# Feed-forward down products of a two-layer decoder: 512-column matmuls written as pairs of 256 columns

## The chip, the cores and the metric

The kernel runs on one core of a Trainium2 chip. Times are device microseconds (us) of that core for one execution of the whole program. The time of the kernel before is the median of three executions, 1899.12 us (1896.09 to 1910.9).

## The reference

Two post-norm decoder layers on 512 tokens of 1024 features. Each layer is a feed-forward network, a mixer (differential attention in layer 0, causal pooling in layer 1), cross-attention into 256 memory tokens, and a second feed-forward network; each of these is followed by a layer norm. What the change touches are the four feed-forward networks:

```python
def swiglu_ffn(x, w_in, w_out):          # x 512 x 1024, w_in 1024 x 5632, w_out 2816 x 1024
    h = x @ w_in
    g, u = jnp.split(h, 2, axis=-1)
    return (jax.nn.silu(g) * u) @ w_out
...
x = layer_norm(a * x + 0.5 * swiglu_ffn(x, ffn_w_in[i, 0], ffn_w_out[i, 0]), ln_g[i, 0], ln_b[i, 0])
```

## The kernel before

Every number is kept as two parts, hi and lo, and every product of float32 is made of three matmuls: hi x hi, hi x lo, lo x hi. The helper `mm3(out, w, x, ...)` issues them in lines 231, 232 and 233; `w` is loaded into the array (stationary, 128 x 128) and `x` streams through it (moving, 128 rows by the columns of `out`). ScalarE makes the hi parts (tiles wh, ha, hb, xh) and VectorE the lo parts (wl and the others), a split each.

A feed-forward network is one block, `ffn`. Its inner features are cut in eleven units of 256, and products of 2 x 2 blocks are made with seven multiplications instead of eight. `up` computes a unit: in each of its steps one of the seven multiplications, 24 matmuls of 256 columns into a bank x, y or z, with the activations moving (xh, xl, xe) and the weights stationary (wh, wl). Units are worked in turns (`FFN_TURNS`): three in turn 0, then two at a time. `down` takes two finished units back to the 1024 features: in each of its seven steps one multiplication, for two groups of 128 tokens (b = 0, 1) and two units (k = 0, 1), so 12 matmuls, each 512 columns wide, into banks px, py and pz. Here the roles are changed: the weights move (wh, wl) and the activations are stationary (ha, hb). In turns 1 to 4 a step of the block is one step of each of two `up`s and one step of `down`, 48 + 12 matmuls. VectorE adds a bank px, py or pz into the tokens X (line 935).

The last three units (`FFN_LAST`) go through `plain_down` without the seven multiplications: for each of 4 groups of tokens and 2 halves of the output's columns a sum of 18 matmuls of 512 columns in a bank ps, with weights moving and activations (xe) stationary. The weights of the first column half lie in wh and wl, those of the second in tiles hb and ha. Its first two sums are begun beside the last two steps of the last `down`, which have no `up` left beside them. The very last sum of the kernel is already made in two halves of 256 columns. After a sum, VectorE adds it to X and the layer norm of that group of tokens begins.

The order on each engine is the one that a list scheduler makes of the code's order and of pairs named by hand: `queue_behind(a, b)` says that instruction a stands behind b. A flag `at_start` marks the kernel's first block. Tiles of activations and of weights are laid 64 bytes apart modulo 512 in the feed-forward and pooling stages (`APART`), so that a moving and a stationary tile begin at different places.

Of the kernel before, what the change touches and what calls it, by code (L numbers as in the profile page):

```python
# [17 lines left out]
P = 128  # L18
D = 1024
S = 512  # L20
# [26 lines left out]
    turn=(1.0, 1.0, 1.2, 1.5),  # L47
# [12 lines left out]
FFN_LAST = (8, 9, 10)  # L60
# [56 lines left out]
def drain(units):  # L117
    for _ in units:
        pass


def few(units, n):
    for _ in range(n):
        next(units, None)


class Trunk:
# [442 lines left out]
    def ffn(self, layer, j, ln, beside=()):  # L570
        w_in, w_out = self.a["ffn_w_in"][layer, j], self.a["ffn_w_out"][layer, j]
        self.seven_of, self.factors = {}, self.factor_tiles()
        nc, n, beside = self.nc, len(FFN_TURNS), iter(beside)
        at_start = bool(self.load_rest)
        downs = {i: self.down(d, w_out, 2.0 * ALPHA if i == 1 else 1.0) for i, (_, d) in enumerate(FFN_TURNS) if d}

        def start(turn):
            ups = FFN_TURNS[turn][0]

            early = (2, 1, 1) if turn == 0 else (0, 0)  # L580
            rest = self.load_rest.pop if turn == 0 and at_start else lambda: lambda: None
            got = [self.up(w_in, u, lane, early[lane], rest() if lane == 0 else None) for lane, u in enumerate(ups)]
            for lane, g in enumerate(got):
                next(g)
                if lane == 1:
                    rest()()
            if turn > 1:
                next(downs[turn])
            return got + [downs[i] for i in downs if i == turn]

        works = start(0)
        if at_start:

            zeros = self.act("hb", (P, P + S), mybir.dt.bfloat16)
            nc.vector.memset(zeros, 0.0)
            idle = self.aux("idle", "yz")
            self.warm(zeros, idle, 7)
            for tag, half in (("px", 0), ("py", 1)):
                for t in self.late[:2]:
                    self.turn(t, half, tag)  # L600
                if half == 0:
                    with self.tc.issue_after(self.last_turn.ins):
                        self.warm(zeros, idle, 9)
                next(works[0])
                if half == 0:
                    next(works[0])
            next(works[1])
        else:
            for w in works + works[:1]:
                next(w)  # L610
            self.turn_late(2)
        self.late = []
        next(works[0])
        act, dve = self.first_split
        if self.begins:

            for late, first in zip(self.begins, (act, dve)):
                self.queue_behind(late, first)
        second = self.second_factors()
        if at_start:  # L620

            next(works[0])
            for w in (works[1], second, second, works[1], works[2], works[2], works[0]):
                with self.behind():
                    next(w)
        else:
            for w in (second, *works[1:], second, downs[1]):
                next(w)
        for turn in range(n):
            behind = turn == n - 1  # L630
            for step in range(1 if turn == 0 else 0, 9 if behind else 7):
                if turn == 0 and (step == 3 or step == 2 and at_start):
                    next(second)
                if step == 4:
                    if behind:
                        coming = [self.plain_down(w_out, layer, j, ln, beside)]
                    else:
                        coming = start(turn + 1)
                        if at_start and turn == 0:
                            with self.tc.issue_after(self.last_load.ins):  # L640
                                next(downs[1])
                if behind and step in (4, 6, 7, 8):
                    next(coming[0])
                if behind and step > 3:
                    few(beside, 2)

                for lane, w in enumerate(works[: None if not behind or step > 1 else -1]):
                    if not (at_start and turn == 0 and lane < 2 and step == 1):
                        next(w, None)
                    if turn == 0 and lane == 1 and step == 2 and at_start:  # L650
                        next(works[0])
                    if turn == 0 and lane == 0 and step == 2 and not at_start:
                        next(second)
                    if at_start and turn == 0 and lane == 0 and step == 3:
                        next(works[2])
                if turn == 1 and step == 3:
                    self.seven_of[self.waiting[0]] = self.seven(self.waiting[1])
            works = coming
        drain(works[0])
# [63 lines left out]
    def up(self, w, u, lane, early, between):  # L723
# [28 lines left out]
        def product(ps, v, a, start=False, passes=False):  # L752
            if passes or between and start and a == 0:
                by_passes(ps, v, a)
                return
            x = self.factors[a]
            for j in range(2):
                o = slice(j * P, (j + 1) * P)
                for k in range(4):

                    self.mm3(
                        ps[:, j], (v[0][:, k, o], v[1][:, k, o]), (x[0][:, k], x[1][:, k]),
                        start and j == k == 0, j == 1 and k == 3, True,
                    )

        def by_passes(ps, v, a, which=range(3)):

            x = self.factors[a]
            halves = [(n, i, l) for n in range(8) for i, l in ((0, 0), (0, 1))]
            for group in ([halves[:8], halves[8:], [(n, 1, 0) for n in range(8)]][w] for w in which):  # L770
                for n, i, l in group:
                    j, k = divmod(n, 4)
                    self.last_mm = nc.tensor.matmul(  # L773
                        ps[:, j], v[i][:, k, j * P : (j + 1) * P], x[l][:, k],
                        start=n == i == l == 0, stop=n == 7 and i == 1, skip_group_check=True,
                    )
# [5 lines left out]
        at_start = early > 0 and self.begins is None  # L782
# [13 lines left out]
        x = bank(self.aux("x", "px") if third else self.mm("x"))  # L796
# [7 lines left out]
        if at_start and lane == 0:  # L804
            by_passes(x, v, 0, (1, 2))
        else:
            product(x, v, 0, True, third and at_start)
# [6 lines left out]
        with self.behind() if at_start else nullcontext():  # L814
            if early > 1 and not at_start:
                wide = v2[0][:, :2].rearrange("p k n -> p (k n)")
                for _ in range(2):
                    nc.tensor.matmul(
                        y.rearrange("p j n -> p (j n)"), v2[0][:, 0, :P], wide, start=True, stop=True
                    )  # L820
            product(y, v2, 1, True, lane != 1 and at_start)
# [47 lines left out]
        if u in FFN_LAST:  # L869
            h = self.act("xe", (P, 2, S)), self.act("xe", (P, 2, S))  # L870
# [25 lines left out]
    def down(self, pairs, w, scale):  # L896
# [14 lines left out]
        hs = [self.seven_of[u] for u in pairs]  # L911

        def operand(raw):
            t = self.hl([P, 2, S])
            self.split(t[0], t[1], raw)
            return [(t[0][:, i], t[1][:, i]) for i in range(2)]
# [4 lines left out]
        def product(ps, b, a, ws, start=False):  # L921

            o = slice(b * P, (b + 1) * P)
            for k in range(2):
                h, l = hs[k][a]
                self.mm3(ps, (h[:, o], l[:, o]), ws[k], start and k == 0, k == 1, not start)

        started = set()

# [8 lines left out]
        ws = operand(b11)  # L938
# [7 lines left out]
        ws = operand(b21)  # L946
        for b in B:
            ps = self.aux("py", "py")
# [3 lines left out]
        ws = operand(b11)  # L952
# [8 lines left out]
        ws = operand(b22)  # L961
# [4 lines left out]
        ws = operand(b11)  # L966
# [5 lines left out]
        ws = operand(b12)  # L972
# [4 lines left out]
        ws = operand(b11)  # L977
# [5 lines left out]
    def plain_down(self, w, layer, j, ln, beside):  # L983
# [8 lines left out]
        ws = [[], []]  # L992
# [15 lines left out]

        def product(ps, half, t, k, n=slice(0, S)):
            o = slice(t * P, (t + 1) * P)  # L1010
            for c in range(2):
                h = [x[:, c, o] for x in self.seven_of[FFN_LAST[k]]]
                self.mm3(ps, h, [x[c][:, n] for x in ws[half][k]], k == c == 0, k == 2 and c == 1)

        operand(0, 0)
        yield
# [2 lines left out]
        for n, (half, t) in enumerate(LAST):  # L1019
# [14 lines left out]
            ps = self.aux("ps", ("yz", "py")[n % 2])  # L1034
# [788 lines left out]
```

## Time and profile before

| | |
|---|---|
| median of three runs | 1899.12 us |
| profiled execution | 1899.25 us, of which the profile's span is 1897.5 us |
| TensorE busy | 1886.5 us, 13120 matmuls |
| weight loads busy | 1730.9 us |
| VectorE busy | 1540.9 us |
| ScalarE busy | 1000.8 us |
| GpSimd busy | 308.2 us |
| memory read and written | 274.79 and 4.19 MB |

Busy times of engines overlap each other. A matmul's busy time contains its pipeline, so that the next one starts before it ends: what a matmul costs in a run of them is the time from its start to the next one's start.

### The profile page before, as it was taken

The page shows a single profiled execution, that of the slowest core. Times are in us where ns is not written, and L with a number is a line of the kernel's source. Part 1 is how long each engine was busy: PE and PEld are TensorE (multiplying, and loading weights), DVE is VectorE, ACT ScalarE, POOL GpSimd, SP SyncE. Part 2 cuts the span into 40 slices and gives each one's busy share as a digit, 9 for nine tenths or more (in the row PEclk, how much of TensorE's full clock was granted, in tenths as well). Part 3 has the DMA queues.
Part 4 walks back from the last instruction along what each step waited for, and adds up shares of the span by engine and source line. Part 5 has one row for each costly group of instructions (what it writes and reads, how often), then busy time and mean ns, then how long its engine had stood idle before and what let it go on. Part 6 is the DMA issues. An engine that isn't in the chain of part 4 may idle for free.

```text
span 1897.5 us, 32589 instructions
## 1 busy us (share of the span) xinstructions
PE 1886.5 (99%) x13120; PEld 1730.9 (91%) x13120; DVE 1540.9 (81%) x2246; ACT 1000.8 (53%) x1542; POOL 308.2 (16%) x274
## 2 busy tenths in 40 slices
PE   9999999999999999999999999999999999999998
PEld 8999998888889988999998999999899889999996
DVE  7888989888876558889887988898786568998886
ACT  6555554566654435555554655555455436555552
POOL 3112120112110002221220311212120012211210
PEclk9999999999999999999999999999999999999999
DMA  9978772322235327987785687777464438867861
GB/s 254 215 178 178 171 141 85 103 69 75 91 112 178 112 70 181 195 177 168 144 188 168 118 179 181 168 166 162 157 172 146 142 69 180 173 159 178 185 129 53
DMA packets 250055, 283.20 MB, mean 149 GB/s; under 512 B 8752, under 2 KB 213040, under 8 KB 249904
## 3 DMA queue, kind: packets, MB, share of 16 engines
q0 software_dynamic: 94080, 94.38, 32.3%
q1 hardware_dynamic: 155824, 186.74, 30.2%
q8 instruction: 103, 1.69, 0.4%
q14 instruction: 48, 0.39, 0.1%
HBM read 274.79 MB, written 4.19 MB: 147 GB/s over the span
## 4 chain that ended last, share of the span: by engine, by line
PE 96%; DMA 2%; DVE 1%; ACT 0%; SPq 0%; issue 0%; POOL 0%; DVEq 0%; ACTq 0%
PE x L231 7%; PE x L232 7%; PE x L233 7%; PE ps L231 5%; PE ps L233 4%; PE ps L232 4%; PE z L231 4%; PE z L233 4%; PE z L232 4%; PE px L233 3%; PE px L231 3%; PE px L232 3%; PE x L773 3%; PE y L231 2%; PE y L232 2%; PE y L233 2%
## 5 line engine op out<-in xcount | busy, mean ns | idle before, releaser
L741 POOL DMA_DIRECT2D ra<-in_ffn_w_in_dram x132 | 170.7, 1307 | 977.6 <-DVE wl L748 960.4
L746 ACT CAST wh<-ra 128x1024 fp32r<-128x1024 f32 x176 | 184.9, 1053 | 197.8 <-PE x L232 63.8
L748 DVE TENSOR_TENSOR wl<-ra,wh 128x1024 fp32r<-128x1024 f32 x176 | 214.2, 1220 | 64.7 <-ACT wh L746 64.0
L231 PE MATMUL x<-xe,wh 128*128 128x256 f32 x704 | 195.0, 277 | 0.0
L232 PE MATMUL x<-xe,wh 128*128 128x256 f32 x704 | 194.8, 277 | 0.0
L233 PE MATMUL x<-xe,wl 128*128 128x256 f32 x704 | 194.8, 277 | 0.0
L746 ACT CAST wh<-rc 128x1024 fp32r<-128x1024 f32 x132 | 138.9, 1053 | 100.3 <-PE x L232 41.6
L143 ACT CAST wh<-b 128x1024 fp32r<-128x1024 f32 x112 | 117.8, 1052 | 134.8 <-PE x L232 62.2
L748 DVE TENSOR_TENSOR wl<-rc,wh 128x1024 fp32r<-128x1024 f32 x132 | 159.5, 1218 | 24.7 <-ACT wh L746 24.7
L144 DVE TENSOR_TENSOR wl<-b,wh 128x1024 fp32r<-128x1024 f32 x112 | 136.7, 1220 | 40.9 <-ACT wh L143 40.9
L231 PE MATMUL x<-xh,wh 128*128 128x256 f32 x536 | 148.7, 277 | 0.0
L232 PE MATMUL x<-xl,wh 128*128 128x256 f32 x536 | 148.4, 277 | 0.0
L233 PE MATMUL x<-xh,wl 128*128 128x256 f32 x536 | 148.4, 277 | 0.0
L231 PEld LDWEIGHTS x<-xe,wh 128*128 128x128 f32 x704 | 132.4, 188 | 1.3
L232 PEld LDWEIGHTS x<-xe,wh 128*128 128x128 f32 x704 | 132.3, 188 | 1.3
L233 PEld LDWEIGHTS x<-xe,wl 128*128 128x128 f32 x704 | 132.2, 188 | 0.0
L144 DVE TENSOR_TENSOR wl<-raw,wh 128x1024 fp32r<-128x1024 f32 x64 | 78.5, 1233 | 45.8 <-ACT wh L143 45.2
L231 PEld LDWEIGHTS x<-xh,wh 128*128 128x128 f32 x536 | 100.8, 188 | 0.7
L232 PEld LDWEIGHTS x<-xl,wh 128*128 128x128 f32 x536 | 100.8, 188 | 0.7
L233 PEld LDWEIGHTS x<-xh,wl 128*128 128x128 f32 x536 | 100.7, 188 | 0.0
L143 ACT CAST wh<-raw 128x1024 fp32r<-128x1024 f32 x64 | 66.4, 1049 | 62.5 <-PE xq L232 18.2
L231 PE MATMUL z<-xe,wh 128*128 128x256 f32 x352 | 97.5, 277 | 0.0
(445 smaller groups left out, 6239.9 us busy)
## 6 DMA issues: line engine op xcount, KB each, us to landing
ra<-in_ffn_w_in_dram POOLq DMA_DIRECT2D x132, 512.0 KB, 7.0
rc<-in_ffn_w_in_dram SPq DMA_DIRECT2D x88, 512.0 KB, 5.8
b<-in_ffn_w_out_dram SPq DMA_DIRECT2D x76, 512.0 KB, 5.0
ra<-in_ffn_w_in_dram SPq DMA_DIRECT2D x44, 512.0 KB, 4.7
rc<-in_ffn_w_in_dram POOLq DMA_DIRECT2D x44, 512.0 KB, 7.3
raw<-in_xa_wkv_dram SPq DMA_DIRECT2D x16, 1024.0 KB, 5.4
raw<-in_da_w_qkv_dram SPq DMA_DIRECT2D x24, 512.0 KB, 3.7
raw<-in_xa_wq_dram SPq DMA_DIRECT2D x8, 1024.0 KB, 5.2
```

The lines of the kernel that those rows point to most:

```text
L143: self.nc.scalar.copy(hi, src),
L144: self.nc.vector.tensor_sub(lo, src, hi.bitcast(F32)),
L231: self.first_mm = mm(out, w[0], x[0], start=start, stop=False, skip_group_check=again)
L232: mm(out, w[0], x[1], start=False, stop=False, skip_group_check=again)
L233: self.last_mm = mm(out, w[1], x[0], start=False, stop=stop, skip_group_check=again)
L741: nc.gpsimd.dma_start(t, source(*block), accum_op=ALU.add)
L746: hi = nc.scalar.copy(v[0], raw)
L748: lo = nc.vector.tensor_sub(v[1], raw, v[0].bitcast(F32))
L773: self.last_mm = nc.tensor.matmul(ps[:, j], v[i][:, k, j * P : (j + 1) * P], x[l][:, k], start=n == i == l == 0, stop=n == 7 and i == 1, s ...
```

## The change

`down` makes each 512-column product as two of 256 columns: all matmuls of the left half first (both units), then those of the right half, in the same bank. `plain_down` does the same with its sums. One down step of each block stays 512 wide, the first one of turn 1 (in the kernel's first block the first one of turn 2 as well): `ahead` marks it. The first matmul of that step is moved: the up product that stands before it is told, from its fourth group of three matmuls on, to stand behind that first matmul, which puts fifteen up matmuls behind it. 1842 of the wide matmuls become 3684 of 256 columns, so the program has 14962 matmuls instead of 13120, and as many more weight loads; 1522 stay wide.

```diff
@@ ffn
+                self.ahead = step == 0 and 0 < turn < 2 + at_start
                 for lane, w in enumerate(works[: None if not behind or step > 1 else -1]):
@@ up: product
             x = self.factors[a]
+            self.up_mms = []
...
                         start and j == k == 0, j == 1 and k == 3, True,
                     )
+                    self.up_mms.append(self.first_mm)
@@ down: product
             o = slice(b * P, (b + 1) * P)
-            for k in range(2):
-                h, l = hs[k][a]
-                self.mm3(ps, (h[:, o], l[:, o]), ws[k], start and k == 0, k == 1, not start)
+            cols = (0, S) if self.ahead else (0, 2 * P, S)
+            for c, e in zip(cols, cols[1:]):
+                for k in range(2):
+                    h, l = hs[k][a]
+                    self.mm3(
+                        ps[:, c:e], (h[:, o], l[:, o]), [w[:, c:e] for w in ws[k]],
+                        start and c == k == 0, k == 1 and e == S, True,
+                    )
+                    if self.ahead and b == k == 0:
+                        self.queue_behind(self.up_mms[-5], self.first_mm)
@@ plain_down: product
             o = slice(t * P, (t + 1) * P)
-            for c in range(2):
-                h = [x[:, c, o] for x in self.seven_of[FFN_LAST[k]]]
-                self.mm3(ps, h, [x[c][:, n] for x in ws[half][k]], k == c == 0, k == 2 and c == 1)
+            for i in range(0, n.stop - n.start, 2 * P):
+                m = slice(n.start + i, n.start + i + 2 * P)
+                for c in range(2):
+                    h = [x[:, c, o] for x in self.seven_of[FFN_LAST[k]]]
+                    self.mm3(
+                        ps[:, i : i + 2 * P], h, [x[c][:, m] for x in ws[half][k]],
+                        k == c == i == 0, k == 2 and c == 1 and m.stop == n.stop, True,
+                    )
```

TensorE's order in a middle down step (the second step of turn 1 in the first block), before. Each row is line, operation, output <- moving, stationary, with the tiles' numbers, and the output's size.

```order
L233 MATMUL y_1092<-xh_86,wl_1094 128x256
L231 MATMUL py_1128<-wh_1124,ha_883 128x512
L232 MATMUL py_1128<-wl_1125,ha_883 128x512
L233 MATMUL py_1128<-wh_1124,ha_884 128x512
L231 MATMUL py_1128<-wh_1124,ha_929 128x512
L232 MATMUL py_1128<-wl_1125,ha_929 128x512
L233 MATMUL py_1128<-wh_1124,ha_930 128x512
L231 MATMUL py_1136<-wh_1124,ha_883 128x512
```

The same place now:

```order
L233 MATMUL py_1128<-wh_1124,ha_884 128x256
L231 MATMUL py_1128<-wh_1124,ha_929 128x256
L232 MATMUL py_1128<-wl_1125,ha_929 128x256
L233 MATMUL py_1128<-wh_1124,ha_930 128x256
L231 MATMUL py_1128<-wh_1124,ha_883 128x256
L232 MATMUL py_1128<-wl_1125,ha_883 128x256
L233 MATMUL py_1128<-wh_1124,ha_884 128x256
```

The bank py_1128 is written by six matmuls of its left half and then by six of its right half, which load the same stationary tiles a second time. The up products before and behind keep their places.

TensorE's order at the first step of turn 1 in the first block (px gathers the down product, x the last up product before it), before:

```order
L231 MATMUL x<-xh,wh 128x256
L232 MATMUL x<-xl,wh 128x256
L233 MATMUL x<-xh,wl 128x256
L231 MATMUL px<-wh,ha 128x512
L232 MATMUL px<-wl,ha 128x512
L233 MATMUL px<-wh,ha 128x512
```

And now:

```order
L231 MATMUL x<-xh,wh 128x256
L232 MATMUL x<-xl,wh 128x256
L233 MATMUL x<-xh,wl 128x256
L231 MATMUL px<-wh,ha 128x512
L231 MATMUL x<-xh,wh 128x256
L232 MATMUL x<-xl,wh 128x256
L233 MATMUL x<-xh,wl 128x256
```

One wide matmul stands between the third and the fourth group of three of that up product; fifteen up matmuls follow it, and then the other eleven wide ones (L232 and L233 of px first).

TensorE's order near the end of the last block, where the second of the sums (ps) is begun and the last `down` comes back to its bank px, before:

```order
L231 MATMUL ps_20795<-wh_20677,xe_20184 128x512
L232 MATMUL ps_20795<-wl_20678,xe_20184 128x512
L233 MATMUL ps_20795<-wh_20677,xe_20185 128x512
L231 MATMUL px_20407<-wh_20777,hb_19564 128x512
L232 MATMUL px_20407<-wl_20778,hb_19564 128x512
```

And now, with other numbers for the same tiles:

```order
L231 MATMUL ps_22505<-wh_22357,xe_21804 128x256
L232 MATMUL ps_22505<-wl_22358,xe_21804 128x256
L233 MATMUL ps_22505<-wh_22357,xe_21805 128x256
L231 MATMUL px_22039<-wh_22475,hb_21100 128x256
L232 MATMUL px_22039<-wl_22476,hb_21100 128x256
```

The scheduler still puts three matmuls of that sum ahead of px and the rest behind its step; they are now three of twelve halves instead of three of six. On VectorE and ScalarE the same instructions stand in a slightly other order within the blocks (a weight split some places ahead of or behind an addition); on GpSimd and SyncE nothing moves.

## The prediction

> **What bounds the kernel now.** I read the page first (busy time, granted clock, the chain that ended last), then what TensorE waited for, then the order of time inside one feed-forward block.
>
> ```profile
> PE 1886.5 (99%) x13120; PEld 1730.9 (91%) x13120; DVE 1540.9 (81%) x2246; ACT 1000.8 (53%) x1542; POOL 308.2 (16%) x274
> PEclk9999999999999999999999999999999999999999
> PE 96%; DMA 2%; DVE 1%; ACT 0%; SPq 0%; issue 0%; POOL 0%; DVEq 0%; ACTq 0%
> ...
> PE idle L138 <- DVE hb L595: 1.3, 1, 1.3
> PE ps L231 <- DVE X L380: 0.8, 1, 0.8
> ```
>
> The last two lines are the longest in the list of TensorE's waits (us in total, times, longest). TensorE is 99% busy at the full clock and holds 96% of the chain. What counts is therefore the spacing of matmul starts, and the change touches exactly that. In the rows below (start in us, length, instruction) the length overlaps its successor, so I divide the time between two starts by the number of matmuls between them. In "x<-xe,wh" xe streams through the array (moving) and wh is loaded into it (stationary).
>
> ```profile
> 85.09 0.39 PE L231 MATMUL py<-wh,ha 128*128 128x512 f32 x1
> ...
> 87.84 0.28 PE L231 MATMUL z<-xh,wh 128*128 128x256 f32 x1
> ...
> 88.54 0.28 PE L231 MATMUL z<-xh,wh 128*128 128x256 f32 x1
> ...
> 93.30 0.39 PE L231 MATMUL pz<-wh,hb 128*128 128x512 f32 x1
> ...
> 232.93 0.39 PE L231 MATMUL px<-wh,hb 128*128 128x512 f32 x1
> ```
>
> One down step, 12 wide matmuls, takes 85.09 to 87.84: 229 ns each. The next six 256-column matmuls take 0.70 us (117 ns each), the following 42 take 4.76 us: 113.3 ns. So a 256-column matmul has two paces here, **quick** (113.3) and **slow** (about 117.7), and after each wide step the up products need some six matmuls to find the quick one. From 85.09 to 232.93 there are 18 such steps of 12 + 48 matmuls, 8.213 us each. In 256-column matmuls at the quick pace a step would be 72 x 113.3 = 8.160 us. **The prize is 0.053 us a step**, half of it in the wide matmuls themselves (2.75 against 2.72 us), half in the six that follow.
>
> **Which pace the new halves take.** This decides the sum, and no split down product stands in the trace. The nearest are the pooled products: 256 columns, with weights moving and activations stationary as in a down step.
>
> ```profile
> 1417.95 0.36 PE L231 MATMUL ps<-wh,pooled 128*128 128x256 f32 x1
> ...
> 1418.39 0.28 PE L231 MATMUL ps<-wh,pooled 128*128 128x256 f32 x1
> ...
> 1421.81 0.28 PE L233 MATMUL ps<-wh,pooled 128*128 128x256 f32 x1
> 1421.92 0.29 PE L231 MATMUL pk<-mem0h,wh 128*128 128x256 f32 x1
> ...
> 1422.17 0.28 PE L233 MATMUL pk<-mem0h,wl 128*128 128x256 f32 x1
> ...
> 1422.51 0.28 PE L233 MATMUL pk<-mem0h,wl 128*128 128x256 f32 x1
> 1422.62 0.28 PE L231 MATMUL ps<-wh,pooled 128*128 128x256 f32 x1
> ...
> 1425.99 0.28 PE L231 MATMUL ps<-wh,pooled 128*128 128x256 f32 x1
> ...
> 1427.36 0.28 PE L231 MATMUL pk<-mem4h,wh 128*128 128x256 f32 x1
> ...
> 1427.71 0.28 PE L231 MATMUL pk<-mem6h,wh 128*128 128x256 f32 x1
> ```
>
> Entered after transposes and a wait (1417.95 has a longer first matmul), 29 of them from 1418.39 to 1421.81 take 117.9 ns each: slow, to the end. Entered from a quick run of pk, 12 of them from 1425.99 to 1427.36 take 1.37 us, 114.2 ns each: quick, with under 0.02 us lost at the seam. So the pace is handed on, not bound to the operands. At the seam back, a slow run becomes quick (1421.92 to 1422.17: 0.25 us for two, then 0.34 for three, about 0.015 us lost in all); the one quick run that returned to pk went on slowly (1427.36 to 1427.71: three in 0.35 us).
>
> Bounds for a pair of halves are then 226.6 ns (quick) and 235.8 (slow) against 229 now: 2.4 won or 6.8 lost on each of the 1842 products that are split. I take the quick end for down steps that lie between up products, since they are entered from 42 quick matmuls without a wait, and the slow end wherever a wait or transposes come before.
>
> A rule of the Trainium skill ("TensorE: Matmul & The Clock Gate", section "Back-to-back issue gap") speaks against the change: columns/2.4 + 2.5 ns per matmul, so a split product would pay one more fixed 2.5 ns. By it 1842 products cost 4.6 us more, an estimate. The row on 1869.03 below bears on it: wide products at their best take 226.7 ns, two quick halves 226.6, so no fixed part is left; and both stand well over the rule's 215.8 and 109.2.
>
> **The tail of a block.** The last of its steps run without up products beside them, and then come the sums.
>
> ```profile
> 1852.31 1.27 DVE L935 SCALAR_TENSOR_TENSOR X<-X,px 128x512 f32<-128x512 f32 x2
> ...
> 1852.79 0.40 PE L233 MATMUL ps<-wh,xe 128*128 128x512 f32 x1
> 1853.14 0.47 PE L231 MATMUL px<-wh,hb 128*128 128x512 f32 x1
> 1853.45 0.40 PE L232 MATMUL px<-wl,hb 128*128 128x512 f32 x1
> ...
> 1869.03 0.39 PE L231 MATMUL ps<-hb,xe 128*128 128x512 f32 x1
> ...
> 1873.11 0.40 PE L231 MATMUL ps<-wh,xe 128*128 128x512 f32 x1
> ...
> 1877.24 0.40 PE L231 MATMUL ps<-hb,xe 128*128 128x512 f32 x1
> ...
> 1881.37 0.40 PE L231 MATMUL ps<-wh,xe 128*128 128x512 f32 x1
> ...
> 1885.51 0.28 PE L231 MATMUL ps<-hb,xe 128*128 128x256 f32 x1
> ...
> 1889.10 0.29 PE L231 MATMUL ps<-ha,xe 128*128 128x256 f32 x1
> ```
>
> At 1853.14 px is written again, and TensorE first waits until VectorE has read it (the first of two additions from 1852.31, 1.27 us together, ends about 1852.95): 0.35 us from 1852.79 where 0.23 would do. Arriving earlier only lengthens that wait. Behind it nothing restores the quick pace: I expect slow halves. The sums of the second column half (hb and ha moving) are dearer still: the only ones already in halves, 30 matmuls from 1885.51 to 1889.10, take 119.7 ns each, 239.4 a pair. Wide, they take 226.7 (18 from 1869.03 to 1873.11) or 229.4 (18 from 1877.24 to 1881.37), 228.1 in the mean. Sums of the first half take 229.4 wide (18 from 1873.11 to 1877.24).
>
> **The change part by part**, against the profiled execution's 1899.25 us (span 1897.5 and 1.75 around it), which is 0.13 above the median 1899.12:
> - Down steps: 7 steps x 4 turns x 4 blocks = 112. Five stay wide; of the others, three a block (12) have no up products behind them, and 95 do. 95 x 0.053, less 0.004 a step for two seams: **-4.7 us**.
> - The first of those three, with the sums begun beside it, ends in the wait above, which eats its gain: 0. The other two, slow: 24 x 117.9 = 2.83 us for 2.75: 8 x 0.08 = **+0.6**.
> - First-half sums behind the wait, about 251: +6.4 ns each: **+1.6**.
> - Second-half sums, 72 in three blocks and 54 in the last, whose final sum was already in halves: 270 x 11.3 ns = **+3.1**.
> - The wide product moved fifteen matmuls ahead, five times: it interrupts an up run, which then needs its six matmuls once more: 5 x 0.026 = **+0.1**. It reads only hi parts; in the first block ScalarE has its wh ready at 70.16, 6.7 us before the step began (76.83), and 1.7 us earlier still finds it there:
>
> ```profile
> 69.12 1.04 ACT L143 CAST wh<-b 128x1024 fp32r<-128x1024 f32 x1
> ...
> 76.83 0.40 PE L231 MATMUL px<-wh,ha 128*128 128x512 f32 x1
> ```
>
> - 1842 more weight loads and matmuls, no DMA, no more work on VectorE or ScalarE. Where additions and splits change places on VectorE, what hides them is the up products. The tightest split in a down step is this one:
>
> ```profile
> 141.09 1.21 DVE L144 TENSOR_TENSOR wl<-b,wh 128x1024 fp32r<-128x1024 f32 x1
> ...
> 142.58 0.39 PE L231 MATMUL py<-wh,ha 128*128 128x512 f32 x1
> 142.81 0.39 PE L232 MATMUL py<-wl,ha 128*128 128x512 f32 x1
> ```
>
> It ends at 142.30, half a us before the matmul that reads it; with halves that one comes 0.12 us sooner, and 0.39 us is left. In the new order this split stands earlier or keeps its place in most turns. Cost 0; without that cover a wait of some 0.3 us would also lose the pace.
>
> Sum: -4.7 + 0.6 + 1.6 + 3.1 + 0.1 = **+0.7 us**, so 1900.0 for such an execution, and 1900 as the median. What the down steps win, the sums give back.
>
> **The rivals.**
> - *Quick everywhere.* The sums, too, come out quick: 521 of them x -2.4 = -1.3, and the middle keeps -4.7: -6 us, **1893**. For it: the pace is handed on. Against: waits and transposes in the tail, and the slow 30 matmuls from 1885.51.
> - *Half the down steps slow.* The seam from up to down isn't alike in all steps (in the address of the stationary tile behind it), and the trace has only two quick seams of one kind. A slow step pays 24 x 4.6 = 0.11 and 0.015 at the way back, where 0.053 went before: +0.07. 48 slow, 47 quick: +1.1, with the tail's 5.4: +6.5, **1906**.
> - *Slower: halves cost 235.8 everywhere.* Place: the down steps; price: +0.07 each, 95 x 0.07 = +6.7, with the tail +12: **1911**. It decides as soon as the pace drops at the first matmul of each step. For it: most rows with weights moving are slow. If each matmul carries a fixed cost, that is its mechanism too. The skill's 2.5 ns, by itself, would make it 1904.
> - *The up products lose it as well*, as at 1427.36: a quick down step, then 48 slow up matmuls (0.22 us), a slow step (0.11), then quick again: +0.24 for two steps, 95/2 x 0.24 = 11.4, with the tail +17: **1916**.
> - *The change isn't there* (the scheduler moves things back): excluded, its order on TensorE shows the halves and the moved product.
>
> **How the numbers follow.** Chances: forecast 0.40, quick everywhere 0.13, half slow 0.17, all slow 0.14, up products slow too 0.09, something else (new waits, other stages entered in another pace) 0.07. Range 1892 to 1912: from quick everywhere to all slow, leaving out the last two, 0.16. A measurement of this kernel tells about 1%, 19 us, from no change (its three runs go from 1896 to 1911). Every case priced above lies within that; over 1% slower takes the up products' case and waits together, 0.06; over 1% faster 0.02, since all the spacing over 113.3 in these parts is some 10 us.
>
> **What would show it.** Middle of a block: steps of 72 matmuls in 8.16 us, with 113.3 in py, pz and px. If those show 118, the third rival; if the matmuls behind them do, the fourth. Tail: ps at 118 (wh moving) and 120 (hb, ha moving); at 113 there, the first rival. The wait before px at the tail longer by 0.05 us. Wrong altogether if TensorE's list shows new waits for VectorE of some us.

## The result and the profile after

The changed kernel takes **1926.24 us** (median; 1924.81 to 1928.94), the kernel before 1897.51 us in the same comparison: ratio 1.0142, 95% interval 1.012 to 1.0163. That is 28.7 us slower, where the prediction said 1900 and at most 1912. The profiled span grew by 27.4 us, from 1897.5 to 1924.9. Of all executions behind the numbers of this document one was far off, 5531 us in the run with 448 bytes below; it enters no ratio.

The page of the changed kernel, in the lines that answer to those shown of before (busy time, granted clock, and the shares of the chain that ended last):

```profile
PE 1906.2 (99%) x14962; PEld 1825.6 (95%) x14962; DVE 1542.0 (80%) x2246; ACT 999.9 (52%) x1542; POOL 308.0 (16%) x274
...
PEclk9999999999999999999999999999999999999999
...
PE 92%; DVE 3%; DMA 2%; issue 1%; ACT 1%; SPq 0%; POOL 0%; DVEq 0%; ACTq 0%; POOLq 0%
```

TensorE is still 99% busy, and its mean granted clock is 0.999 in both profiled executions. VectorE now holds 3% of the chain where it held 1%, and TensorE's waits have new names at the top (us in total, times, longest):

```profile
PE px L231 <- DVE X L945: 2.3, 4, 1.3
PE ps L232 <- DVE wl L144: 1.9, 2, 1.3
PE pp L1443 <- DVE pooled L144: 1.3, 2, 0.7
PE ps L232 <- DVE hb L144: 1.3, 1, 1.3
```

To see where the 27.4 us stand, I cut both traces at the same matmuls (first down product of a block, first up product behind the step that stays wide, last down steps, end of the sums) and subtract:

| after minus before, us | block 1 | block 2 | block 3 | block 4 | sum |
|---|---|---|---|---|---|
| ahead of the down steps: stages between blocks, turn 0, the wide step | +1.0 | +0.3 | +2.4 | +4.6 | +8.2 |
| middle: the steps of turns 1 to 4 with up products | +3.3 | +2.8 | +2.8 | +2.8 | +11.6 |
| tail: the last down steps and the sums | +2.6 | +1.3 | +2.5 | +1.1 | +7.5 |

About 18 of the 27.4 us are pace, that is spacing of matmul starts without a wait: the middles (11.6), the first turn of block 3 (2.4) and some 3.9 of the tails. The rest is waits and the smaller pieces of the first row. The +1.0 there for block 1 can't be put down to the change: up to that block's first sum the kernel with the down steps alone (below) has the same instructions in the same order on every engine, and it shows -1.1. In its profiled execution 242 matmuls late in turn 0 take 27.43 us, 113.3 ns each; the same 242 take 28.50 us in that of the changed kernel, 117.8 each.

**The middle.** The timeline of TensorE in the first block (start in us, length, instruction), the first matmul of each run:

```profile
83.35 0.28 PE L231 MATMUL y<-xh,wh 128*128 128x256 f32 x1
...
86.07 0.28 PE L231 MATMUL py<-wh,ha 128*128 128x256 f32 x1
...
88.79 0.28 PE L231 MATMUL z<-xh,wh 128*128 128x256 f32 x1
...
94.45 0.28 PE L231 MATMUL pz<-wh,hb 128*128 128x256 f32 x1
...
97.28 0.28 PE L231 MATMUL z<-xe,wh 128*128 128x256 f32 x1
...
102.73 0.28 PE L231 MATMUL pz<-wh,hb 128*128 128x256 f32 x1
...
105.45 0.28 PE L231 MATMUL x<-xe,wh 128*128 128x256 f32 x1
```

24 up products to 86.07 take 113.3 ns each, and the 24 halves of the down step to 88.79 take 113.3 too: the step is entered quick and stays quick. But the 48 up products behind it (to 94.45) take 117.9, and the next 24 halves (to 97.28) 117.9. Then 48 up products to 102.73 take 113.5, the first of them slow, and the next halves 113.3. Steps go **two by two**, quick and slow. Two of them, 88.79 to 105.45, take 16.66 us; two of before take 16.43.

**The wide product that moved ahead**, first block:

```profile
134.58 0.28 PE L231 MATMUL x<-xh,wh 128*128 128x256 f32 x1
...
136.34 0.40 PE L232 MATMUL px<-wl,ha 128*128 128x512 f32 x1
...
138.88 0.28 PE L231 MATMUL y<-xh,wh 128*128 128x256 f32 x1
```

The fifteen up products behind it, quick before, take 1.76 us, 117.3 each; the eleven remaining wide matmuls take 231 each.

**The tail**, last block:

```profile
1878.84 0.28 PE L233 MATMUL ps<-wh,xe 128*128 128x256 f32 x1
1879.45 0.36 PE L231 MATMUL px<-wh,hb 128*128 128x256 f32 x1 [0.34 <-DVE X L945]
...
1885.99 0.28 PE L231 MATMUL ps<-wh,xe 128*128 128x256 f32 x1
...
1891.43 0.28 PE L231 MATMUL ps<-hb,xe 128*128 128x256 f32 x1
...
1895.75 0.28 PE L231 MATMUL ps<-hb,xe 128*128 128x256 f32 x1
```

From start to start the gap before px is 0.61 us. A quick half needs 0.11 of that, so 0.50 is wait. Before it was 0.35 behind a wide matmul, which needs 0.23: a wait of 0.12. Behind the wait the first two sums are quick (48 in 5.44 us, 113.3), and the sums of the second half are at 120.0 (36 in 4.32). Blocks 2 and 3 begin their tails alike; in block 1, whose tail is entered slowly, those 48 take 117.8 each.

**Ahead of block 4** most of the loss is no pace but a wait: in layer 1's pooling stage TensorE waits, in four gaps that hold 3.5 us beyond its usual spacing, for VectorE's splits, VectorE for ScalarE's, and ScalarE for a weight from memory. The same cast of that weight on ScalarE, before:

```profile
1396.34 1.05 ACT L143 CAST wh<-raw 128x1024 fp32r<-128x1024 f32 x1 [3.10 <-DMA raw<-in_xa_wkv_dram]
```

and after:

```profile
1420.53 1.05 ACT L143 CAST wh<-raw 128x1024 fp32r<-128x1024 f32 x1 [8.90 <-DMA raw<-in_xa_wkv_dram]
```

ScalarE stands idle 8.90 us for it instead of 3.10.

### The profile page after: what moved, and what is told of

Same layout as the page of the kernel before. It is cut to its first block, busy times and chain, and to the rows that moved or that the text cites. A ratio compares the mean times of both kernels' runs of the same rounds, so it can differ in the third digit from the quotient of the medians.

```text
span 1924.9 us, 36256 instructions
## 1 busy us (share of the span) xinstructions
PE 1906.2 (99%) x14962; PEld 1825.6 (95%) x14962; DVE 1542.0 (80%) x2246; ACT 999.9 (52%) x1542; POOL 308.0 (16%) x274
## 4 chain that ended last, share of the span: by engine, by line
PE 92%; DVE 3%; DMA 2%; issue 1%; ACT 1%; SPq 0%; POOL 0%; DVEq 0%; ACTq 0%; POOLq 0%
PE x L232 7%; PE x L231 7%; PE x L233 7%; PE ps L231 4%; PE ps L232 4%; PE ps L233 4%; PE z L232 4%; PE z L231 4%; PE z L233 4%; PE px L231 3%; PE px L233 3%; PE px L232 3%; PE x L776 3%; PE y L231 2%; PE y L232 2%; PE y L233 2%
## 5 line engine op out<-in xcount | busy, mean ns | idle before, releaser
L233 PE MATMUL x<-xe,wl 128*128 128x256 f32 x704 | 196.1, 279 | 0.0
L232 PE MATMUL x<-xe,wh 128*128 128x256 f32 x704 | 196.1, 279 | 0.0
L143 ACT CAST wh<-b 128x1024 fp32r<-128x1024 f32 x112 | 117.9, 1053 | 137.0 <-PE x L232 68.0
L233 PE MATMUL x<-xh,wl 128*128 128x256 f32 x536 | 149.4, 279 | 0.0
L232 PE MATMUL x<-xl,wh 128*128 128x256 f32 x536 | 149.4, 279 | 0.0
L233 PEld LDWEIGHTS x<-xe,wl 128*128 128x128 f32 x704 | 132.4, 188 | 0.0
L232 PEld LDWEIGHTS x<-xe,wh 128*128 128x128 f32 x704 | 132.2, 188 | 0.0
L231 PE MATMUL px<-wh,hb 128*128 128x256 f32 x384 | 107.1, 279 | 2.3 <-DVE X L945 2.3
L233 PE MATMUL px<-wh,hb 128*128 128x256 f32 x384 | 106.5, 277 | 0.0
L232 PE MATMUL px<-wl,hb 128*128 128x256 f32 x384 | 106.5, 277 | 0.0
```

Of the source, the lines that this page charges most:

```text
L143: self.nc.scalar.copy(hi, src),
L231: self.first_mm = mm(out, w[0], x[0], start=start, stop=False, skip_group_check=again)
L232: mm(out, w[0], x[1], start=False, stop=False, skip_group_check=again)
L233: self.last_mm = mm(out, w[1], x[0], start=False, stop=stop, skip_group_check=again)
```

## The experiments

All are compared with the kernel before on the same chip. "Theory" in the expectations is: a 256-column matmul runs at one of two paces, about 113.3 and 117.7 ns, and hands its pace on.

**Down steps alone.** The changed kernel with the sums wide again.

```diff
@@ plain_down: product (back as before)
+            for c in range(2):
+                h = [x[:, c, o] for x in self.seven_of[FFN_LAST[k]]]
+                self.mm3(ps, h, [x[c][:, n] for x in ws[half][k]], k == c == 0, k == 2 and c == 1)
```

> The changed kernel with the last output sums left 512 columns wide; only the down steps are in halves (one step of each block wide, first product fifteen ahead). Theory (the pace is handed from matmul to matmul, and a quick down step hands a slow one to the up products behind it): the middles of the blocks take 216.3 us each as in the changed kernel (213.5 before), alternating 113 and 118 ns from step to step, +11 to +12 us in all; the tails return to about 40.5, 40.4, 39 and 38.7 us plus 0.2 each; total 1909 to 1915. Rival (each product in halves carries a fixed cost, 27 us / 1842 = 15 ns): 1284 products cost +19 us, 1916 to 1918, spread evenly over the steps. Second rival (the loss sits in new waits for VectorE): the middles stay at 213.5 and the total comes near 1900.

1915.66 us, ratio 1.0085 (1.0068 to 1.0101). The alternation is there without the halved sums:

```profile
96.20 0.28 PE L231 MATMUL z<-xe,wh 128*128 128x256 f32 x1
...
101.86 0.28 PE L231 MATMUL pz<-wh,hb 128*128 128x256 f32 x1
...
104.69 0.28 PE L231 MATMUL x<-xe,wh 128*128 128x256 f32 x1
```

48 up products in 5.66 us and 24 halves in 2.83: 117.9 both. Middles +2.8 us a block as after, in the first block +4.4 with a new wait before py (a start-to-start gap of 1.2 us). Tails +4.0 in sum, half of it one longer wait before px in the first block (a 2.5 us gap, 0.5 before). The time is a little over the theory's range, by those waits. It is just under the range of the rival with a fixed cost, so the time alone doesn't decide against it. The rows do: that rival spreads its cost evenly over the steps, and these go from 113.4 to 117.9 and back.

**Sums alone.** The kernel before, its sums in halves.

```diff
@@ plain_down: product
+            for i in range(0, n.stop - n.start, 2 * P):
+                m = slice(n.start + i, n.start + i + 2 * P)
...
+                        ps[:, i : i + 2 * P], h, [x[c][:, m] for x in ws[half][k]],
```

> The kernel before with only the last output sums in halves; down steps wide, no product moved. Theory: the middles stay at 213.46 us; the tails grow by 1.1 to 1.4 us each from the pace (118 ns with weights of the first half moving, 120 with those of the second), since nothing brings the quick pace back behind the wait for VectorE; whether the waits in the tails and in the pooling stage of layer 1 (about 3 and 4 us in the changed kernel) come from these sums too is open: total 1902 without them, 1909 with them. Rival (fixed cost of 15 ns a product): 558 products, +8 us, 1905 to 1906, with no product at its old 227 to 229 ns a pair.

1915.77 us, ratio 1.0094 (1.0074 to 1.0113): far over both. Tails +5.6 in sum. The rest stands elsewhere: block 3, which is the same as before up to its sums, is slow from its beginning (+2.4 ahead of its down steps, +5.6 in its middle), and the stages ahead of block 4 lose 4.1. Block 3, TensorE:

```profile
1131.00 0.28 PE L231 MATMUL y<-xh,wh 128*128 128x256 f32 x1
...
1136.65 0.40 PE L231 MATMUL py<-wh,ha 128*128 128x512 f32 x1
...
1139.42 0.28 PE L231 MATMUL z<-xh,wh 128*128 128x256 f32 x1
```

48 up products at 117.7 and 12 wide ones at 231, step after step: 8.42 us where before took 8.213. So the kernel before has a slow course of its own: here a wide step entered slowly hands the slow pace on, and all steps of the block stay there. That isn't so for every wide step entered slowly: the first one of the kernel before (76.83 to 79.63, 233 each) is entered at 118 too, and the up products behind it are quick after four. Block 3 follows block 2 at once, and its turn 0 stood at 117.8 here and after the full change too.

**Another distance.** The changed kernel with `APART` 256 in place of 64 in the feed-forward stage.

```diff
-APART, ROUND, LINE = {"ffn": 64, "da": 448, "pool": 64}, 512, 480
+APART, ROUND, LINE = {"ffn": 256, "da": 448, "pool": 64}, 512, 480
```

> The changed kernel with tiles of activations and weights laid 256 bytes apart modulo 512 in the feed-forward stages, not 64, so that a moving tile stands as far from a stationary one in a down step as in an up product. Theory (the seam is one-sided because the distance is 64 one way and 448 the other): the alternation goes; all middle steps have one pace, 113 (middles near 211.5 us, total 1915 or less) or 118 throughout (middles near 219, total 1935). Rival (the seam loses the pace whatever the distance, because there a weight tile follows itself at the same place): steps still alternate, middles 216 us, total about 1925.

1968.51 us, ratio 1.0363 (1.0348 to 1.0379).

```profile
90.17 0.28 PE L231 MATMUL z<-xh,wh 128*128 128x256 f32 x1
...
95.93 0.28 PE L231 MATMUL pz<-wh,hb 128*128 128x256 f32 x1
...
98.81 0.28 PE L231 MATMUL z<-xe,wh 128*128 128x256 f32 x1
```

48 up products in 5.76 us, 24 halves in 2.88: **120.0 ns all of them**, up and down alike, no alternation. One pace was expected, this value was not. The instructions and their order are the same on every engine and only addresses moved, so where tiles lie sets the pace. That it is the moving tile's place against the stationary one's is the nearest reading. The edit also moves both against tiles that other engines use, and no run kept these apart. 120.0 is also what the tail's hb and ha products take, whose tiles begin 0 apart from xe (modulo 512).

**Second token group wide.** Down steps alone, each step's second group (b = 1) left wide, so that wide matmuls stand ahead of the up products.

```diff
-            cols = (0, S) if self.ahead else (0, 2 * P, S)
+            cols = (0, S) if self.ahead or b == 1 else (0, 2 * P, S)
```

> As the first of these (sums wide), and in each down step only the first group of 128 tokens is in halves; the second group's six matmuls stay 512 wide, so that up products follow a wide matmul as before. Theory: the halves are entered from quick up products and take 113.3 ns, the up products behind need six matmuls for the quick pace as before, so a step gains 14 ns: middles 213.1 us, total 1 to 2 us below before (1895 to 1897). Rival (halves cost more by themselves): 642 products in halves x 7 to 15 ns, +4 to +10 us.

1899.68 us, ratio 1.0005 (0.9995 to 1.0014).

```profile
841.67 0.28 PE L231 MATMUL px<-wh,hb 128*128 128x256 f32 x1
...
843.03 0.39 PE L231 MATMUL px<-wh,hb 128*128 128x512 f32 x1
...
844.40 0.28 PE L231 MATMUL x<-xh,wh 128*128 128x256 f32 x1
...
849.87 0.28 PE L231 MATMUL px<-wh,hb 128*128 128x256 f32 x1
```

Twelve halves at 113.3, six wide at 228, and the up products are back at 114.0 in the mean: the alternation is gone, and the middles of blocks 2 to 4 are 0.32 us each *under* before, the gain the theory gave. So splitting costs nothing here by itself; the seam from halves back to up products does. The first block lost 1.4 in its middle and 1.3 in its tail to new waits for VectorE, hence the miss of the range.

**The same in every step**, with no step wholly wide and none moved ahead.

```diff
-                self.ahead = step == 0 and 0 < turn < 2 + at_start
+                self.ahead = False
```

> Every down step of the kernel before, its first token group (b = 0) in halves and its second (b = 1) wide; no step wholly wide, no product moved ahead, sums wide as before. Theory (the pace is handed on, and a wide group at a step's end is what lets the up products behind it settle on the quick pace): 12 halves at 113.4 ns in each step in the place of 6 wide matmuls at 229, 0.014 us a step, so the middle of each block some 0.33 us shorter, and with VectorE's order as before 1896 to 1897. Rival (the halves themselves bring the first block's waits for VectorE that the run with the moved step showed, 1.5 us before py and 1.3 us before px): 1898 to 1900.

1898.95 us, ratio 0.9998 (0.9989 to 1.0008). Middles -0.32 us in all four blocks, -1.3 together; the first block's tail takes back 0.8 and the stages behind it 1.0, while 0.7 is won ahead of the first down step, where executions of the same instructions differ by more than that. The total lies in the rival's range and not in the theory's. The theory had the pace right; of the rival's two waits the one before px came (a gap of 1.28 us, 0.50 before), the one before py did not. The wait in that tail is this one:

```profile
297.19 0.36 PE L231 MATMUL px<-wh,hb 128*128 128x256 f32 x1 [0.88 <-DVE X L945]
```

So the best use of halves found here equals the kernel before and doesn't beat it.

**First token group wide** instead of the second.

```diff
-            cols = (0, S) if self.ahead else (0, 2 * P, S)
+            cols = (0, S) if self.ahead or b == 0 else (0, 2 * P, S)
```

> Down steps with the first token group wide and the second in halves (the other way round than in the run with the second group wide); the one step of each block wide and moved, sums wide. Theory (what stands at the step's end decides what the up products behind it do): halves behind wide matmuls are slow, as the 30 halves behind the wide sums at the kernel's end were, and slow halves hand the up products the quick pace: 12 x 117.8 for 6 x 229 ns, some 0.02 us a step more than before, 1899 to 1902. If the halves settle on the quick pace behind the wide ones, all 48 up products behind each step are slow, 0.2 us a step: 1917 to 1920. Rival (only the number of halves counts, not which group has them): up products quick and halves quick, 1897 to 1900, as with the second group wide.

1913.03 us, ratio 1.0072 (1.0048 to 1.0095).

```profile
94.74 0.28 PE L231 MATMUL pz<-wh,hb 128*128 128x256 f32 x1
...
96.10 0.28 PE L231 MATMUL z<-xe,wh 128*128 128x256 f32 x1
...
101.75 0.40 PE L231 MATMUL pz<-wh,hb 128*128 128x512 f32 x1
...
103.16 0.28 PE L231 MATMUL pz<-wh,hb 128*128 128x256 f32 x1
...
104.57 0.28 PE L231 MATMUL x<-xe,wh 128*128 128x256 f32 x1
...
110.02 0.39 PE L231 MATMUL px<-wh,hb 128*128 128x512 f32 x1
```

As many halves as with the second group wide, but two by two again: halves 113.3, up products 117.7, six wide at 235, halves 117.5, and then up products at 113.5. What stands last in the step decides, so the rival that only counts halves falls. My own forecast (halves behind wide ones are slow) falls as well: in this run wide matmuls hand on the pace that they got. The forecast's other case (halves quick, and the up products behind every step slow) holds for every other step only.

**The roles exchanged.** The changed kernel with 448 bytes in place of 64: up products then have the distance that down products had, and the other way round.

```diff
-APART, ROUND, LINE = {"ffn": 64, "da": 448, "pool": 64}, 512, 480
+APART, ROUND, LINE = {"ffn": 448, "da": 448, "pool": 64}, 512, 480
```

> The changed kernel with the feed-forward tiles of activations and weights 448 bytes apart modulo 512 in the place of 64, so that the roles of the one that comes first are exchanged. Theory (a seam between up and down products drops or lifts the pace by the order in which the two tiles lie): steps still go two by two between 113 and 118 ns, with the drop now at the other seam (into the down step or back), 1918 to 1932. Rival (each distance has one pace of its own, as 256 bytes had 120 ns): one pace for all and no alternation, 1893 if it is 113 ns, 1950 if it is 118.

1930.39 us, ratio 1.0155 (1.0132 to 1.0179).

```profile
94.26 0.28 PE L231 MATMUL pz<-wh,hb 128*128 128x256 f32 x1
...
96.99 0.28 PE L231 MATMUL z<-xe,wh 128*128 128x256 f32 x1
...
102.43 0.28 PE L231 MATMUL pz<-wh,hb 128*128 128x256 f32 x1
...
105.26 0.28 PE L231 MATMUL x<-xe,wh 128*128 128x256 f32 x1
...
110.92 0.28 PE L231 MATMUL px<-wh,hb 128*128 128x256 f32 x1
```

Halves quick (24 in 2.73 us), up products behind them still quick (48 in 5.44); then the drop: halves 117.9, up products 117.9 (5.66). **The drop has moved to the seam into the down step**, and the seam back holds. The theory gave that, and the time. The time holds 1.5 us of another kind: in the first block's tail, behind a gap of 2.35 us before px, the granted clock is 0.50 from 304.8 to 308.2, and fifteen halves take 213 ns each.

**Both on the same side.** The changed kernel with ha and hb 128 bytes on, so that the moving tile has the same distance from the stationary one (-64) in up and in down products. The same edit was made to two more kernels: all down steps in halves with wide sums, and the kernel before, all wide.

```diff
@@ phase_pool
+                elif t == "_h":
+                    self.pad(ctx, 2 * self.apart)
@@ ffn_phase
-        bufs = dict(b1=1, b3=1, b2=1, b4=1, _x=0, xe=6, hb=4, sp=4, ha=4, sr=1, hr=3)
+        bufs = dict(b1=1, b3=1, b2=1, b4=1, _x=0, xe=6, _h=0, hb=4, sp=4, ha=4, sr=1, hr=3)
```

> The changed kernel with the down products' stationary tiles (ha, hb) laid 128 bytes on instead of 0, modulo 512, so that the moving tile lies 64 bytes behind the stationary one in up products and in down products alike; before, it lay 64 bytes behind in up products and 64 ahead in down products. Theory (the pace changes only at a seam where that order turns over, as the runs with 64 and with 448 bytes showed at opposite seams): no alternation inside a block; 72 matmuls of a step all at 113.3 ns, middles 5 us under the kernel before instead of 11.6 over it, 1906 to 1912 in all; if a block is entered slowly and nothing turns it over, it is slow to the end, 7 us a block, up to 1945. Rival (the seams' drop comes from the change of operands, not from where they lie): two by two as before, 1924 to 1928.

> The same laying of ha and hb (128 bytes on), all down steps in halves without a wide or a moved one, and the sums wide as in the kernel before. Theory: steps of 8.16 us, middles 5 us under the kernel before, of which the first block's waits for VectorE take back 1 to 3: 1893 to 1896. Slow throughout: 1920 to 1928. Rival (the operands, not where they lie): two by two, 1913 to 1917 like the run with the down steps alone.

> The kernel before, all wide, with the same laying of ha and hb (128 bytes on). Theory: without a seam that turns over, the up products behind a wide step need no six matmuls to find the quick pace: 0.026 us a step, some 2.6 us in all, 1894 to 1896; if the pace is slow at a block's start it stays slow, wide matmuls too, 5.6 us a block, up to 1920. Rival (the six slow matmuls come from the wide ones, not from where the tiles lie): no change, 1897 to 1899.

1919.23 us (ratio 1.0107, 1.0092 to 1.0123), 1909.82 (1.0059, 1.0046 to 1.0072) and 1915.20 (1.0087, 1.0073 to 1.0101). The first of them (the added lines shift the line numbers by two):

```profile
96.25 0.29 PE L233 MATMUL z<-xe,wh 128*128 128x256 f32 x1
...
101.71 0.28 PE L233 MATMUL pz<-wh,hb 128*128 128x256 f32 x1
...
104.54 0.29 PE L233 MATMUL x<-xe,wh 128*128 128x256 f32 x1
```

48 up products at 113.8, 24 halves at 117.9, in *every* step: now both seams turn the pace, down at the way in, up at the way back, and a middle is 1.75 us over before (2.98 in the first block). Where down steps are in halves with wide sums, the middles are 1.76 over in each block, the same. The all wide kernel, whose instructions are those of before:

```profile
92.42 0.39 PE L233 MATMUL pz<-wh,hb 128*128 128x512 f32 x1
...
95.21 0.28 PE L233 MATMUL z<-xe,wh 128*128 128x256 f32 x1
...
100.87 0.39 PE L233 MATMUL pz<-wh,hb 128*128 128x512 f32 x1
...
103.67 0.28 PE L233 MATMUL x<-xe,wh 128*128 128x256 f32 x1
...
109.13 0.39 PE L233 MATMUL px<-wh,hb 128*128 128x512 f32 x1
```

12 wide in 2.79 us, 48 up at 117.9, 12 wide in 2.80, then 48 up at 113.8 to the next step: the wide kernel alternates two by two when ha and hb lie elsewhere, and there a wide step doesn't hand on the pace that it got: entered quick it is left slow, and the other way round. My refined theory (the pace turns only where the order of the two tiles turns over) falls: no run kept one pace through a block, and all three times are over its ranges for a quick course. (The first time holds 1.5 us at a granted clock of 0.50 in the first block's tail, as the run with 448 bytes does.) Its rival, that only the change of operands counts and not where they lie, falls as well, since moving the tiles changed which steps are slow. What stays is that addresses decide at which seam the pace turns; by which rule was not found.

**Block 3's sums wide**, all else as in the changed kernel.

```diff
+            size = n.stop - n.start if (layer, j) == (1, 0) else 2 * P
-            for i in range(0, n.stop - n.start, 2 * P):
+            for i in range(0, n.stop - n.start, size):
```

> The changed kernel with the sums of the third block alone wide again (layer 1's first feed-forward network, ahead of the pooling stage). Theory (those halved sums move the third block's end against the loads of the pooling stage, and the weights of the next stage then land later): the waits of TensorE for VectorE in the pooling stage go, 4 us, and about 1.2 us of the block's tail: 1920 to 1922. Rival (the waits come from all that is late before, whatever the sums of that block are): 1924 to 1926.

1920.00 us, ratio 1.0106 (1.0087 to 1.0126): the theory's range. The stages ahead of block 4 go from +4.6 to -0.2, block 3's tail from +2.5 to +0.5, and ScalarE gets its weight after the old wait:

```profile
1412.37 1.05 ACT L143 CAST wh<-raw 128x1024 fp32r<-128x1024 f32 x1 [2.98 <-DMA raw<-in_xa_wkv_dram]
```

So those waits belong to the halved sums of that one block. The weight is not asked for late: its transfer is issued 18.8 us later than before in the changed kernel, and block 3 ends 18.9 us later. But it takes 14.5 us from issue to landing, where it takes 9.1 before and 9.0 in this run. That it takes longer because it shares the transfers' time with others that now start closer to it is my reading of the trace. It wasn't tried by itself.

## Why the prediction was wrong, point by point

- **The step that failed: "I take the quick end for down steps that lie between up products, since they are entered from 42 quick matmuls without a wait"**, with 0.004 us for the seams. Its first half held: a step entered quick is quick. The 42 quick matmuls ahead of it are what didn't hold. The seam back, from quick halves to up products, drops the pace, and the 48 up products and the next step are then slow. Middles: -4.7 forecast, +11.6 measured. Why the pace drops at that seam stays open: the runs show that addresses decide at which seam it does, and not the rule.
- **The fourth rival was the right mechanism**, with its price: +0.24 for two steps, measured 16.66 - 16.43 = 0.23; +11.4 for the middles, measured +11.6. The row at 1427.36 showed just this drop, and that at 1421.92 the recovery. I had booked both as the cost of a seam, 0.004 us a step, and not as the pace of all that follows; and gave the rival 0.09 because one seam of another stage bore it, though the forecast rested on no more.
- **The cost of a fixed part in each matmul**, the rule weighed against the change: 12 quick halves and 6 wide in the second-group kernels give -0.32 us a block. The Trainium skill ("TensorE: Matmul & The Clock Gate", section "Back-to-back issue gap") would make them dearer by 2.5 ns for each split product, an estimate of +0.4 us for the 24 steps of a middle with six such products each; the trace disagrees. The section gives that gap for an isolated matmul, not for a stream like this one.
- **The tail**: +5.3 by pace forecast. Measured +7.5, of which about 3.6 are longer waits for VectorE (gaps of TensorE before px and before a sum with hb, less the spacing of the matmul ahead of each, against the same in before) and some 3.9 pace. hb and ha at 120 came as forecast. "Behind it nothing restores the quick pace" was wrong in blocks 2 to 4, where 48 halves behind the wait ran at 113.3.
- **The wait before px**: 0.05 us longer forecast, 0.38 measured in the last block (0.50 against 0.12), and in the first block a gap of 1.6 us where before has 0.5. The sign that the prediction named last, new waits for VectorE of some us, came too: the four rows of TensorE's waits above hold 6.8 us. An earlier arrival alone doesn't explain the gap in the first block: there VectorE's order put the addition from px later as well.
- **The stages outside the down steps and the sums**, for which the sum has no term, cost 8.2 us: 4.6 ahead of block 4, where the weight of the pooling stage lands late, 2.4 for block 3's turn 0, which goes at 117.8 behind block 2's halved sums (the sums-alone kernel has it, the downs-alone kernel hasn't), and 1.2 ahead of blocks 1 and 2, of which the 1.0 of block 1 isn't shown to come from the change.
- **The moved product**: +0.1 for five forecast, about 0.5 by the rows. It slows fifteen up products and the eleven wide ones behind, about 0.1 each (block 3 with the down steps alone is 0.09 over before there).
- **The range** ended at 1912 because it left out the up products' rival and "other stages entered in another pace" together. Both came in one kernel. The parts don't simply add: the down steps alone cost 16.6 us and the sums alone 16.7, the whole change 28.7.

## What to carry to other kernels

Before a run of matmuls is cut differently, look at start-to-start times on *both* sides of every seam and follow them over two periods: a gain in the changed instructions can set the pace of those behind them, which are twice as many in a step here (48 against 24). Treat a pace as something the program is in, set by history and addresses. The kernel before keeps the quick one only as long as its tiles lie as they do, and one block that was entered slowly (block 3 with the sums alone) stayed slow to its sums. And where a tail shifts by a few us, look at the loads of the next stage, since a late transfer can cost more than the tail itself.

## What the hardware showed that I had not expected

- A matmul of the same size on the same engine at the same granted clock (a mean of 0.998 to 0.999 in every profiled execution here) takes 113.3, 117.7 or 120.0 ns for 256 columns, and some 229 or 233 for 512, by what ran before and by where tiles lie: 64 or 448 bytes apart (modulo 512) gave the first two, 256 and 0 the third. At 128 apart, the sums with hb in the same-side run, it is 118.6 in the mean.
- Moving only ha and hb by 128 bytes, with no other change to the kernel before, cost 0.87% (0.73 to 1.01).
- At 64 bytes a slow run of halves turns the up products quick at the seam back within four matmuls; at 448 they stay slow (105.26 to 110.92). A slow wide step did either: the block stayed slow in the sums-alone kernel and turned quick at the first step of the kernel before.
- The same instructions in the same order took either pace in two executions (113.3 and 117.8 ns at the end of block 1's turn 0).
- The granted clock can fall to 0.50 behind one wait and not behind a longer one: it did for 3.4 us behind gaps of 2.35 us in two runs (448 bytes, and same side with halved sums), and didn't behind gaps of 2.5 us (down steps alone) and 3.0 us (same side, down steps).
